# Join's transposed blocks in the tile that also holds the right side of the solve and the state sum, and a fourth buffer for second parts of weights

## Chip, cores and metric

The kernel runs on one core of a Trainium2 chip. A core has five engines that run side by side: TensorE (PE; its weight loads are PEld), VectorE (DVE), ScalarE (ACT), GpSimd (POOL) and SyncE (SP, which here issues DMAs only). Each takes its instructions in the order in which the built program lists them. The metric is the device time of one execution in microseconds (us), as a median of several runs.

## What is computed

A two-layer decoder trunk on x of 1024 tokens by 1024 channels, all in float32. The first layer mixes over time by the RWKV-7 recurrence, the second by sliding-window attention; each layer is followed by a squared-ReLU MLP with 4096 hidden channels. The change touches the recurrence:

```python
def step(S, inp):
    r_t, w_t, k_t, v_t, a_t, b_t = inp
    sa = jnp.einsum('bhvk,bhk->bhv', S, a_t)
    S = S * w_t[:, :, None, :] + sa[..., None] * b_t[:, :, None, :] + v_t[..., None] * k_t[:, :, None, :]
    y = jnp.einsum('bhvk,bhk->bhv', S, r_t)
    return S, y
...
def squared_relu_mlp(h, w1, w2):
    return jnp.square(jax.nn.relu(h @ w1)) @ w2
```

## The kernel before

**Products.** A float32 product of the projections, MLPs and attention is made of three products of parts (`mm3`, L132 to L136): each operand is split into a first part, rounded on ScalarE (L129), and a second part, the rest, subtracted on VectorE (L130). For a weight, `weight` (L265) loads 128x512 raw values into a tile with the tag `wr`, and writes the first part into a tile `wh` and the second into a tile `wl`. A tile tag has a fixed number of buffers (L45 to L47: 5 for `wr`, 4 for `wh`, 3 for `wl`), taken in turn: the next tile of a tag may be written once everything that reads the old tile in that buffer is done. An activation's two parts go to tiles `m2k`; in the projections each activation comes out of a mix of two tokens (`shifted`, L347, whose VectorE rows are L353 and L358 and write `relu`), and its second part is subtracted on VectorE or on GpSimd.

**Recurrence.** It is worked in chunks of 64 tokens. The 1024 tokens and 16 heads make 16 units of 128 tokens (two chunks, c = 0 and 1) by 8 heads (L806). A unit goes through these steps, whose order within the program is given by short strings (L53 to L55, L817):

- `prep` and `inner` (L574, L627) make decayed keys and the matrices of a chunk: AR, BK, and RT with XT, the blocks of a triangular matrix that has to be inverted. Of each 64x64 matrix, four 32x32 blocks, XT holds the transpose; its block at the second 32 rows and first 32 columns is not used by anybody.
- `solve` (L669) inverts the diagonal 32x32 blocks, 31 dependent pairs of steps on GpSimd (L680, L682), and brings the results through memory into RT (DMAs of L684, L689).
- `join` (L693) fills in the off-diagonal blocks: two VectorE transposes (L700), products on TensorE (L705), copies on ScalarE into the tile AT (L707), products (L711), copies into RT.
- `chunks` (L716) carries the state through the two chunks: products with the state SV (L743, L748), `pb` copied by ScalarE (L745), the solve's products with `pb` and RT (L752) copied into SV (L754), the sum of the state, `sn` (L757, L759), and from it SV for the second chunk (L762) and the state itself (L763).
- `finish` (L770) normalizes and stores.

`join` of a unit stands last in its string, behind `chunks` of the unit before it. But the build has a scheduler: it orders each engine's instructions by their priority and by when it reckons that their operands are ready, within what data and buffers allow. The recurrence is given priority (L810); the projections, and later the first MLP, supply the work around it.

**Stages** (times in the profile of before): projections with the first units up to about 656 us, the output product of the time mix to about 820 us, the first MLP with the last units to about 1230 us, then the queries and attention beside MLPs, and a pure MLP from about 2110 us to the end.

Of the kernel before, what the change touches and what calls it, by code (L numbers as in the profile page):

```python
# [10 lines left out]
F32 = mybir.dt.float32  # L11
# [8 lines left out]
P = 128  # L20
# [7 lines left out]
D = 64  # L28
L = 64
TB = 128  # L30
NC = TB // L
GP = 4
# [3 lines left out]
B = 32  # L36
# [7 lines left out]
M2K = 24  # L44
WR = 5  # L45
WH = 4
WL = 3  # L47
ROWS = 4
STG = 3
RELU = 3  # L50
# [24 lines left out]
class Trunk:  # L75
# [25 lines left out]
    def t(self, pool, tag, shape, dt=F32, bufs=1):  # L101
        return pool.tile(shape, dt, tag=tag, name=self.nm(tag), bufs=bufs)
# [162 lines left out]
    def weight(self, ap, shape, gain=None):  # L265
# [3 lines left out]
        nc.sync.dma_start(raw, ap)  # L269
        hi, lo = self.t(self.mp, "wh", shape, F32R, WH), self.t(self.mp, "wl", shape, F32R, WL)  # L270
        if gain is None:
# [103 lines left out]
    def lora_out(self, W2, u, off, dst, pt):  # L375
# [7 lines left out]
        for o in range(KT):  # L383
            if o % 4 == 0:
                raw = self.t(self.mp, "wr", [P, 512], F32, WR)
                for r0 in (0, 64):
                    nc.sync.dma_start(raw[r0:r0 + 64], W2[:, o * P:o * P + 512])
                wh, wl = self.t(self.mp, "wh", [P, 512], F32R, WH), self.t(self.mp, "wl", [P, 512], F32R, WL)
                nc.scalar.copy(wh, raw)
# [303 lines left out]
    def join(self, made):  # L693

        nc = self.nc
        AR, BK, RT, EL, bonus, XT, Xs = made
        n = NQ // 2
        sides = [(hp, self.sides(hp)[1].start, self.sides(hp)[2].start) for hp in range(2)]
        for hp, b, k in sides:
            nc.vector.transpose(XT[b:b + B, :, 0:B], RT[k:k + B, hp, :, 0:B])  # L700
        AT = self.t(self.rp, "AT", [P, n, B], F32)
        ps = self.turn().rearrange("p (q i) -> p q i", i=B)
        for q in range(n):
            for hp, b, k in sides:
                nc.tensor.matmul(ps[k + B:k + L, q], XT[b:b + B, q, B:], XT[b:b + B, q, 0:B], start=True, stop=True)  # L705
        for hp, b, k in sides:
            nc.scalar.copy(AT[k + B:k + L], ps[k + B:k + L, 0:n])  # L707
        ps = self.turn().rearrange("p (q i) -> p q i", i=B)
        for q in range(n):
            for hp, b, k in sides:  # L710
                nc.tensor.matmul(ps[k:k + B, q], AT[k + B:k + L, q], RT[k + B:k + L, hp, q, B:], start=True, stop=True)  # L711
        for hp, b, k in sides:
            nc.scalar.copy(RT[k:k + B, hp, :, B:], ps[k:k + B, 0:n])
        return AR, BK, RT, EL, bonus

    def chunks(self, blk, g, made):  # L716

        nc = self.nc
        t = lambda tag, shape, bufs=1, dt=F32: self.t(self.rp, tag, shape, dt, bufs)
        pt, t0 = PART[blk]  # L720
        AR, BK, RT, EL, bonus = made
        SV = t("SV", [P, NC, 2, GP, D])
        sides = [(hp, *self.sides(hp)[1:]) for hp in range(2)]
        heads = [(pi, *x) for pi in range(GP) for x in sides]
        dV = self.dV[pt][t0:t0 + TB, g * GH * D:(g + 1) * GH * D]
        for hp, bs, ks in sides:
            for c in range(NC):
                nc.sync.dma_start(SV[ks, c, hp], dV[c * L:(c + 1) * L].rearrange("l (r h d) -> l h r d", h=2, d=D)[:, hp])
            nc.vector.tensor_copy(SV[bs, 0, hp], self.state[g][bs])
        bv = t("bv", [P, NC, GH, D])  # L730
        nc.sync.dma_start(bv[L:].rearrange("l c h d -> l c (h d)"), dV.rearrange("(c l) d -> l c d", l=L))
        nc.gpsimd.tensor_tensor(bv[L:], bv[L:], bonus[L:].unsqueeze(3).broadcast_to([L, NC, GH, D]), ALU.mult)
        y = t("y", [P, GP, NC, L])

        def bank():
            return self.turn().rearrange("p (h d) -> p h d", d=D)[:, 0:GP]

        S = self.state[g]
        for c in range(NC):
            el = EL[:, :, c].unsqueeze(2).broadcast_to([P, GP, D])  # L740
            ps = bank()
            for pi, hp, bs, ks in heads:
                nc.tensor.matmul(ps[ks, pi], AR[:, hp, pi * NC + c, L:], SV[:, c, hp, pi], start=True, stop=True)  # L743
            pb = t("pb", [P, GP, D])
            nc.scalar.copy(pb, ps)  # L745
            py = bank()
            for pi, hp, bs, ks in heads:
                nc.tensor.matmul(py[bs, pi], SV[:, c, hp, pi], AR[:, hp, pi * NC + c, 0:L], start=True, stop=True)  # L748
            nc.scalar.copy(y[:, :, c], py)
            ps = bank()  # L750
            for pi, hp, bs, ks in heads:
                nc.tensor.matmul(ps[bs, pi], RT[ks, hp, pi * NC + c], pb[ks, pi], start=True, stop=True)  # L752
            for hp, bs, ks in sides:
                nc.vector.tensor_copy(SV[bs, c, hp], ps[bs])  # L754
            ps = bank()
            for pi, hp, bs, ks in heads:
                nc.tensor.matmul(ps[bs, pi], BK[:, pi * NC + c, hp], SV[:, c, hp, pi], start=True, stop=True)  # L757
            sn = t("sn", [P, GP, D])
            nc.vector.tensor_tensor(sn, ps, S, ALU.add)  # L759
            if c < NC - 1:  # L760
                for hp, bs, ks in sides:
                    nc.vector.tensor_tensor(SV[bs, c + 1, hp], sn[bs], el[bs], ALU.mult)  # L762
            nc.vector.tensor_tensor(S, sn, el, ALU.mult)  # L763
            py = bank()
            for pi, hp, bs, ks in heads:
                nc.tensor.matmul(py[bs, pi], SV[bs, c, hp, pi], RT[bs, hp, pi * NC + c], start=True, stop=True)
            nc.vector.tensor_tensor(y[:, :, c], y[:, :, c], py, ALU.add)
        return y, bv
# [355 lines left out]
```

## Time and profile before

| | us |
|---|---|
| median of 3 runs | 2679.01 |
| lowest and highest | 2678.21, 2679.69 |
| the profiled execution | 2679.98 |
| its span, first to last instruction | 2678.3 |
| TensorE busy | 2541.7 (95%) |
| VectorE busy | 1700.6 (63%) |
| ScalarE busy | 1306.1 (49%) |
| GpSimd busy | 621.2 (23%) |
| mean granted TensorE clock | 0.972 of full |

Busy times are sums over one execution on the chip. An engine that waits is not busy; the trace says for most waits which instruction's end released it, and "issue" where it shows none. TensorE's clock has two levels, 1.2 and 2.4 GHz; a granted clock of 0.97 over a stretch is the mean of the two there.

### The profile page before, as it was taken

The numbers are of one execution on the slowest core, as the hardware profiler recorded it, in microseconds if no ns is written. First come the engines' busy times: TensorE is split into PE (matmuls) and PEld (weight loads), VectorE is DVE, ScalarE is ACT, GpSimd is POOL, SyncE is SP. The second block draws the span as 40 slices with busy tenths as digits, with TensorE's granted clock in tenths as the row PEclk, the third lists the DMA queues.
The fourth block names the chain that finished last, engine by engine and source line by source line (L and its number), as shares of the span: only waits on it lengthen the run. The fifth ranks groups of instructions, "written<-read, shape, count | busy, mean of one in ns | idle before, by whom it ended". The sixth has DMA issues, their size and how long they took to land.

```text
span 2678.3 us, 43154 instructions
## 1 busy us (share of the span) xinstructions
PE 2541.7 (95%) x15166; PEld 2054.0 (77%) x15166; DVE 1700.6 (63%) x3235; ACT 1306.1 (49%) x2702; POOL 621.2 (23%) x1221
## 2 busy tenths in 40 slices
PE   6978988998889999999999999999999999999999
PEld 4767766766767777777887888888888888888887
DVE  8578778656666666645567885445899644444433
ACT  5555566464444444333455665335666533434342
POOL 6176744740454444420010000001000000000000
PEclk9989989899889999999999999999999999999999
DMA  5656643654644444333424454342446433333332
GB/s 177 196 173 177 184 115 113 179 143 151 177 105 114 120 122 117 109 107 119 140 87 151 126 153 123 95 154 89 138 142 196 123 103 96 121 91 105 96 99 95
DMA packets 440635, 349.64 MB, mean 131 GB/s; under 512 B 97105, under 2 KB 360417, under 8 KB 440417
## 3 DMA queue, kind: packets, MB, share of 16 engines
q1 hardware_dynamic: 423008, 344.77, 43.1%
q10 hardware_dynamic: 17408, 2.10, 0.5%
q8 instruction: 120, 1.97, 0.3%
q14 instruction: 99, 0.80, 0.1%
HBM read 280.71 MB, written 57.67 MB: 126 GB/s over the span
## 4 chain that ended last, share of the span: by engine, by line
PE 50%; DVE 3%; DMA 2%; ACT 1%; issue 1%; SPq 0%; DVEq 0%; ACTq 0%
PE big L134 16%; PE big L135 16%; PE big L136 16%; DMA dS<-sc 1%; DMA row<-dS 1%; DVE wl L130 0%; DVE sc L975 0%; DVE sc L978 0%; DMA wr<-in_mlp_w 0%; PE sm L1001 0%; PE sq L955 0%; PE sm L1002 0%; PE sq L956 0%; PE big L252 0%; SPq L983 0%
## 5 line engine op out<-in xcount | busy, mean ns | idle before, releaser
L129 ACT CAST wh<-wr 128x512 fp32r<-128x512 f32 x741 | 458.0, 620 | 853.4 <-PE big L136 435.5
L130 DVE TENSOR_TENSOR wl<-wr,wh 128x512 fp32r<-128x512 f32 x741 | 527.3, 716 | 474.5 <-issue 223.4
L134 PE MATMUL big<-m2k,wh 128*128 128x512 f32 (+3 forms) x1528 | 578.6, 381 | 12.2 <-ACT m2k L129 4.6
L135 PE MATMUL big<-wl,m2k 128*128 128x512 f32 (+1 forms) x1472 | 578.4, 394 | 9.4 <-DVE wl L130 7.6
L135 PE MATMUL big<-m2k,wh 128*128 128x512 f32 (+2 forms) x1528 | 572.7, 376 | 6.4 <-POOL m2k L130 4.3
L136 PE MATMUL big<-m2k,wl 128*128 128x512 f32 (+2 forms) x1528 | 571.8, 377 | 5.1 <-DVE wl L130 5.1
L136 PE MATMUL big<-wh,m2k 128*128 128x512 f32 (+1 forms) x1472 | 566.9, 392 | 3.0 <-POOL m2k L130 3.0
L134 PE MATMUL big<-wh,m2k 128*128 128x512 f32 (+1 forms) x1472 | 512.1, 394 | 11.3 <-ACT m2k L129 7.7
L134 PEld LDWEIGHTS big<-m2k,wh 128*128 128x128 f32 (+1 forms) x1528 | 292.0, 192 | 76.1 <-issue 6.3
L135 PEld LDWEIGHTS big<-wl,m2k 128*128 128x128 f32 x1472 | 281.3, 191 | 72.2 <-DVE wl L130 13.5
L136 PEld LDWEIGHTS big<-m2k,wl 128*128 128x128 f32 (+1 forms) x1528 | 292.0, 191 | 58.1 <-DVE wl L130 7.7
L135 PEld LDWEIGHTS big<-m2k,wh 128*128 128x128 f32 (+1 forms) x1528 | 291.7, 191 | 57.8 <-POOL m2k L130 7.0
L134 PEld LDWEIGHTS big<-wh,m2k 128*128 128x128 f32 x1472 | 279.9, 191 | 73.0 <-ACT m2k L129 9.1
L136 PEld LDWEIGHTS big<-wh,m2k 128*128 128x128 f32 x1472 | 280.4, 191 | 59.3 <-POOL m2k L130 3.6
L680 POOL TENSOR_TENSOR tmp<-Xs,TT 128x60 f32<-128x60 f32 (+24 forms) x496 | 197.2, 398 | 143.2 <-DMA Xs<-dXs 106.7
L130 DVE TENSOR_TENSOR m2k<-relu,m2k 128x512 fp32r<-128x512 f32 (+1 forms) x200 | 135.1, 678 | 119.6 <-ACT m2k L129 119.2
L682 POOL TENSOR_TENSOR TT<-TT,tmp 128x60 f32<-128x60 f32 (+24 forms) x496 | 195.1, 393 | 37.8
L129 ACT CAST m2k<-relu 128x512 fp32r<-128x512 f32 (+1 forms) x272 | 146.6, 545 | 45.8 <-DVE relu L353 33.4
L322 DVE TENSOR_TENSOR b<-b,big 128x512 f32<-128x512 f32 x192 | 124.7, 680 | 8.8 <-PE big L136 8.2
L223 POOL TENSOR_TENSOR ss<-ss,mhalf 128x4 f32<-128x4 f32 (+1 forms) x10 | 8.9, 888 | 453.8 <-DVE ss L222 453.8
L223 POOL TENSOR_TENSOR qn<-qn,mhalf 128x8 f32<-128x8 f32 x16 | 27.1, 1692 | 373.8 <-DVE qn L222 290.4
L314 ACT ACTIVATE relu<-relu 128x512 f32<-128x512 f32 x128 | 80.9, 633 | 3.5
(229 smaller groups left out, 3089.6 us busy)
## 6 DMA issues: line engine op xcount, KB each, us to landing
wr<-in_mlp_w SPq DMA_DIRECT2D x512, 256.0 KB, 2.7
wr<-in_a_w_rkv SPq DMA_DIRECT2D x144, 256.0 KB, 3.2
ld<-dP SPq DMA_DIRECT2D x16, 1024.0 KB, 6.8
dS<-sc SPq DMA_DIRECT2D x28, 512.0 KB, 2.8
row<-dS SPq DMA_DIRECT2D x112, 128.0 KB, 3.0
dP<-stg SPq DMA_DIRECT2D x64, 128.0 KB, 3.4
AR<-RA SPq DMA_DIRECT2D x32, 256.0 KB, 4.4
Xs<-dXs SPq DMA_DIRECT2D x64, 128.0 KB, 2.7
```

Source lines behind the costliest of these rows:

```text
L129: self.nc.scalar.copy(hi, src)
L130: (engine or self.nc.vector).tensor_tensor(lo, src, hi.bitcast(F32), ALU.subtract)
L134: mm(ps, ah, bh, start=start, stop=False)
L135: mm(ps, ah, bl, start=False, stop=False)
L136: mm(ps, al, bh, start=False, stop=stop)
L223: nc.gpsimd.tensor_tensor(dst, dst, self.mhalf[:, :n], ALU.pow)
L314: nc.scalar.activation(r, r, AF.Square)
L322: nc.vector.tensor_tensor(v, v, ps[tt], ALU.add)
L680: nc.gpsimd.tensor_tensor(v, Xs[:, k:k + 1, k + 1:].broadcast_to([P, m, n]), TT[:, 0:m, k:k + 1].broadcast_to([P, m, n]), ALU.mult)
L682: nc.gpsimd.tensor_tensor(TT[:, 0:m, k + 1:], TT[:, 0:m, k + 1:], v, ALU.add)
```

## The change

Three edits. `join` writes its two transposes into a new tile TX, with the tag `pb`, of which there is one buffer; the sum `sn` of `chunks` gets the same tag, so `pb`, the sum and TX follow each other in one buffer. The transposes are no longer put into XT; the products of L705 (now L707) read TX and XT. AT is not a tile of its own any more but the unused block of XT. The two tags that are gone (`sn` and AT, 1 KB in each partition each) make room for a fourth `wl` buffer of 2 KB. Lines from L700 on stand one or two further down in the change (L700 is L701, L743 is L745, L759 is L761, L762 is L764).

```diff
-WL = 3
+WL = 4
...
+        TX = self.t(self.rp, "pb", [P, n, B], F32)
         for hp, b, k in sides:
-            nc.vector.transpose(XT[b:b + B, :, 0:B], RT[k:k + B, hp, :, 0:B])
-        AT = self.t(self.rp, "AT", [P, n, B], F32)
+            nc.vector.transpose(TX[b:b + B], RT[k:k + B, hp, :, 0:B])
+
+        AT = XT[:, :, 0:B]
         ps = self.turn().rearrange("p (q i) -> p q i", i=B)
         for q in range(n):
             for hp, b, k in sides:
-                nc.tensor.matmul(ps[k + B:k + L, q], XT[b:b + B, q, B:], XT[b:b + B, q, 0:B], start=True, stop=True)
+                nc.tensor.matmul(ps[k + B:k + L, q], XT[b:b + B, q, B:], TX[b:b + B, q], start=True, stop=True)
...
-            sn = t("sn", [P, GP, D])
+            sn = t("pb", [P, GP, D])
```

**What it does to the order.** First VectorE, in the unit of the first of five alike (beside the first MLP). Before, from the first chunk's sum on; RT_9682 and XT_9683 belong to the next unit, SV_9559 and states to this one:

```order
L759 TENSOR_TENSOR sn_9611<-sq_9602,states 128x256
L700 STREAM_TRANSPOSE XT_9683<-RT_9682 32x8x32
L767 TENSOR_TENSOR y_9569<-y_9569,sq_9616 128x4x64
L762 TENSOR_TENSOR SV_9559<-sn_9611,EL_8584 64x256 x2
L763 TENSOR_TENSOR states<-sn_9611,EL_8584 128x256
L130 TENSOR_TENSOR wl_12471<-wr_12468,wh_12470 128x512
L700 STREAM_TRANSPOSE XT_9683<-RT_9682 32x8x32
L130 TENSOR_TENSOR wl_12497<-wr_12494,wh_12496 128x512
```

Now, from the same sum on:

```order
L761 TENSOR_TENSOR pb_9611<-sq_9602,states 128x256
L764 TENSOR_TENSOR SV_9559<-pb_9611,EL_8584 64x256 x2
L765 TENSOR_TENSOR states<-pb_9611,EL_8584 128x256
L769 TENSOR_TENSOR y_9569<-y_9569,sq_9616 128x4x64
L130 TENSOR_TENSOR wl_12471<-wr_12468,wh_12470 128x512
```

SV and the state now follow the sum at once. The transposes stand further on, here from the second chunk's sum:

```order
L761 TENSOR_TENSOR pb_9667<-sq_9658,states 128x256
L130 TENSOR_TENSOR wl_12551<-wr_12548,wh_12550 128x512
L769 TENSOR_TENSOR y_9569<-y_9569,sq_9670 128x4x64
L731 COPY SV_9974<-states 64x256 x2
L648 TENSOR_TENSOR RT_10097<-sm_10099,maskg 64x256
L765 TENSOR_TENSOR states<-pb_9667,EL_8584 128x256
L648 TENSOR_TENSOR RT_10097<-sm_10100,maskg 64x256
L701 STREAM_TRANSPOSE pb_9933<-RT_9682 32x256 x2
L592 COPY EL_10266<-ec_10262 128x8
L130 TENSOR_TENSOR wl_12574<-wr_12571,wh_12573 128x512
```

Both transposes now stand directly behind the second chunk's last use of its sum. Of the 16 joins, 8 had their first transpose ahead of the second chunk's sum before (the seventh, the eighth and the last six); in the change none has.

Second, TensorE at the same unit in the change, where the second chunk's first products begin:

```order
L135 MATMUL big_12412<-wl_12435,m2k_12318 128x512
L136 MATMUL big_12412<-wh_12434,m2k_12319 128x512
L745 MATMUL sq_9626<-SV_9559,AR_9265 64x64
L134 MATMUL big_12410<-wh_12452,m2k_12362 128x512
L745 MATMUL sq_9626<-SV_9559,AR_9265 64x64 x7
L750 MATMUL sq_9637<-AR_9265,SV_9559 64x64 x8
```

Between the last product of L759, which the first chunk's sum reads, and the first of L745 stand the eight small products of L768 and 20 products of the MLP.

Third, VectorE near the start of the program, in the projections (`relu` is the mix of two tokens, `wl` a weight's second part), as a piece of the difference:

```order
 L477 COPY hlast<-b_8_188 128x8
+L130 TENSOR_TENSOR wl_372<-wr_369,wh_371 128x512
 L468 COPY b_367_1551<-hlast 128x8
 L353 SCALAR_TENSOR_TENSOR relu_250<-m2k_221,vec,b_8_188 128x256
```

The fourth `wl` of the program moved ahead of six rows of L353, and the fifth moved up alike. Such shifts by a few rows go through all of the program.

## Rows read from the trace of the kernel before

**Rows 1.** The page: busy time, share of the span and instructions of each engine.

```profile
PE 2541.7 (95%) x15166; PEld 2054.0 (77%) x15166; DVE 1700.6 (63%) x3235; ACT 1306.1 (49%) x2702; POOL 621.2 (23%) x1221
```

**Rows 2.** Busy times in stages: stretch, length, PE, PEld, DVE, ACT, POOL, clock, DMA.

```profile
0.00:656.00 656.00, 572.18 (x4429) 444.86 (x4430) 479.23 (x935) 372.48 (x832) 331.13 (x642) 0.92 0.55 160
...
820.00:1130.00 310.00, 294.83 (x2295) 234.10 (x2294) 203.48 (x376) 122.44 (x238) 134.96 (x309) 0.99 0.42 114
...
2110.00:2678.00 568.00, 562.90 (x2488) 464.02 (x2486) 242.74 (x373) 218.81 (x365) 1.01 (x1) 1.00 0.33 100
```

**Rows 3.** Waits of TensorE from 820 to 1130 us: total, times, longest.

```profile
PE sq L743 <- issue: 12.0, 5, 2.8
```

**Rows 4.** VectorE in order of time, 1085 to 1097 us: start, length, idle before.

```profile
1085.62 0.69 DVE L130 TENSOR_TENSOR m2k<-relu,m2k 128x512 fp32r<-128x512 f32 x1 [1.54 <-ACT m2k L129]
1086.34 0.42 DVE L759 TENSOR_TENSOR sn<-sq,states 128x256 f32<-128x256 f32 x1
1093.97 0.43 DVE L700 STREAM_TRANSPOSE XT<-RT 32x256 f32<-32x256 f32 x1 [7.21 <-DMA RT<-dTT]
...
1094.78 0.86 DVE L762 TENSOR_TENSOR SV<-sn,EL 64x256 f32<-64x256 f32 x2
```

**Rows 5.** TensorE in order of time, at the same unit.

```profile
1095.29 0.24 PE L743 MATMUL sq<-SV,AR 128*64 128x64 f32 x1 [2.79 <-issue]
...
1132.89 0.69 PE L705 MATMUL sq<-XT 32*32 32x32 f32 x32
```

**Rows 6.** VectorE in order of time, 602 to 605 us.

```profile
602.71 0.43 DVE L700 STREAM_TRANSPOSE XT<-RT 32x256 f32<-32x256 f32 x1 [6.39 <-DMA RT<-dTT]
...
604.67 0.87 DVE L754 COPY SV<-sq 64x256 f32<-64x256 f32 x2
```

**Rows 7.** TensorE in order of time, at 605 us.

```profile
605.14 0.33 PE L757 MATMUL sq<-SV,BK 128*64 128x64 f32 x2 [1.72 <-DVE SV L754]
```

**Rows 8.** VectorE at the end of the second chunk of the unit of rows 4.

```profile
1107.98 0.42 DVE L763 TENSOR_TENSOR states<-sn,EL 128x256 f32<-128x256 f32 x1
```

**Rows 9.** GpSimd in order of time, the last steps of the solve.

```profile
1085.74 0.69 POOL L680 TENSOR_TENSOR tmp<-Xs,TT 128x42 f32<-128x42 f32 x1
1086.51 0.27 POOL L682 TENSOR_TENSOR TT<-TT,tmp 128x42 f32<-128x42 f32 x1
1086.86 0.26 POOL L680 TENSOR_TENSOR tmp<-Xs,TT 128x35 f32<-128x35 f32 x1
...
1089.68 0.21 POOL L682 TENSOR_TENSOR TT<-TT,tmp 128x8 f32<-128x8 f32 x1
```

**Rows 10.** The tile tmp, 820 to 1130 us: ns, shortest/median/longest.

```profile
L680 POOL TENSOR_TENSOR tmp<-Xs,TT x142: 208/294/1292, 820.5 to 1129.4; 128x60 f32<-128x60 f32 x12, 128x48 f32<-128x48 f32 x10, 128x28 f32<-128x28 f32 x10, 128x54 f32<-128x54 f32 x9
```

**Rows 11.** Waits of TensorE over the whole span: total, times, longest.

```profile
PE big L134 <- ACT m2k L129: 12.3, 5, 5.1
...
PE big L135 <- DVE wl L130: 7.6, 11, 1.2
PE big L136 <- DVE wl L130: 5.1, 6, 2.3
...
PE big L135 <- DVE wl L275: 1.8, 2, 0.9
...
PE big L394 <- DVE wl L390: 0.7, 1, 0.7
```

**Rows 12.** Waits of TensorE in the first 100 us.

```profile
PE big L135 <- DVE wl L130: 5.5, 8, 1.2
```

**Rows 13.** Busy times near the start (columns as in rows 2).

```profile
28.00:56.00 28.00, 22.50 (x88) 15.33 (x88) 28.00 (x35) 15.56 (x36) 23.11 (x24) 1.00 0.45 133
```

**Rows 14.** The tile wl on VectorE, 0 to 656 us: ns, shortest/median/longest.

```profile
L130 DVE TENSOR_TENSOR wl<-wr,wh x163: 482/693/2031, 12.0 to 653.5; 128x512 fp32r<-128x512 f32 x154, 128x480 fp32r<-128x480 f32 x6, 128x320 fp32r<-128x320 f32 x3
```

**Rows 15.** Busy times in two later stretches of 65 us (columns as in rows 2).

```profile
886.00:951.00 65.00, 62.12 (x481) 49.12 (x478) 43.66 (x80) 26.42 (x52) 28.77 (x63) 0.97 0.42 114
951.00:1016.00 65.00, 61.76 (x500) 48.95 (x498) 44.09 (x81) 26.45 (x53) 30.01 (x67) 1.00 0.44 119
```

## The prediction, before the change was run

> **What bounds the kernel now.** I read the page first. TensorE is busy for 95% of the span and VectorE for 63% [rows 1]. The busy times by stage place what is lost [rows 2]: from 0 to 656 us (projections) TensorE is idle for 84 us at a mean clock of 0.92; in the last 568 us it is idle for 5 us. So a change can only win before about 1300 us, by closing gaps in TensorE's work. There is one regular series of gaps: from 820 to 1130 us, while the first MLP runs beside the recurrence, TensorE is idle for 15.2 us in all, and 12.0 us of that is five waits in front of L743, the first product of a chunk [rows 2, 3]. Those rows name no releaser ("issue"), so I looked at VectorE around the last of them [rows 4]. It finishes the state sum of a unit's first chunk at 1086.76, and the next row in its order is join's first transpose for the *next* unit, which waits 7.21 us for the DMA that brings the solved blocks. Behind it stand the two instructions (L762) that write SV for the second chunk. They need nothing but the sum, yet start at 1094.78; TensorE, which had reached L743, resumes at 1095.29 after a gap of 2.79 us [rows 5]. So these gaps are order on VectorE, not work.
>
> **The change part by part.**
>
> *TX in the tile of the sums.* TX has the tag of the sums and one buffer, so no transpose may be written while a sum of the unit before it is still to be read; its last reader is L763 on VectorE itself. The scheduler must thus put both transposes behind the second chunk's L763, as the order of the change shows. In 8 of the 16 joins they stood ahead of it before, the five with gaps among them. With SV straight behind the sum, SV is there some 1.3 us after the sum begins (0.42 for it, 0.86 for the two copies [rows 4]); in the new order 20 products of the MLP stand on TensorE between the end of L759 and L745, some 4.5 us at the 0.226 us for each in the pure MLP (562.90 us for 2488 [rows 2]), so TensorE should not wait. I take the five gaps as gone: **-12.0 us**. The full amount reaches the end, since from 820 us on TensorE has little other idle time. One earlier join has the same fault on another instruction: at 602.71 the transposes that had waited for the DMA hold up the copy at L754, and TensorE stands 1.72 us at L757 [rows 6, 7]: **-1.7 us**.
>
> What does the wait cost in its new place? Shifted forward, the second chunk ends its sums at 1086.8 + (1107.98 - 1094.78) = 1100.0 [rows 4, 8], and the solved blocks had landed by 1093.97: 6 us to spare. The join's products start only at 1132.89 [rows 5], so they are not delayed. Nor does sharing cost a wait across engines: `pb` of a chunk follows join's first products in TensorE's order anyhow, and the sum follows the products that read `pb`. Zero, covered by these distances.
>
> The spare has an enemy: VectorE no longer stands idle under the end of the solve. While VectorE subtracted two tiles in SBUF (the L130 row of [rows 4]) a 128x42 step on GpSimd took 0.69 us, the next step of that size 0.27 [rows 9]. The ten steps behind the sum, 1086.86 to 1089.89, take 0.26 falling to 0.21 us each [rows 9], 2.3 in all; at 0.69 each they take 6.9 and the blocks land 4.6 us later, still inside the 6 us. At the longest step seen, 1.29 us [rows 10], they would not. The Trainium skill, GPSIMD Engine Reference, section 1. Specifications, says that GpSimd shares its SBUF interfaces with VectorE and contends with VectorE instructions that have two SBUF inputs; by that rule the wait comes back, which is the second rival. The trace agrees as to the slowing, not as to its size.
>
> *AT in the unused block of XT.* Same two copies, same sizes, and XT has two buffers; it is held until join's second products instead of the first, with the unit's next user two units away. Zero.
>
> *Fourth `wl` buffer.* No instruction is added. It lets VectorE split a weight one tile further ahead. TensorE's direct waits on `wl` bound what that can win: 7.6 + 5.1 + 1.8 + 0.7 = 15.2 us [rows 11]. Of these at least 5.5 us lie in the first 100 us [rows 12], where VectorE has no idle time from 28 to 56 us [rows 13]: there a tile made earlier pushes the activations behind it later, and I give nothing for it. Of the other 9.7 us I take a third, **-3.2 us**, because several stand behind a VectorE that was held by something else. Bounds: 0 and -15.2; and below, since an order that favours weights can also starve the activations (last rival).
>
> *The clock.* Two stretches of 65 us that hold one of the five gaps each ran at 0.97 and at 1.00 [rows 15]: gaps of this size did not pull the clock down as a rule, and I take 0 for it. The Trainium skill, TensorE: Matmul & The Clock Gate, section HAM oscillation, holds that idle gaps of TensorE also drop its clock; by that the closed gaps would give back more, an estimate of 2 us (3% of 65) wherever it happens, or 10 us over five. In the projections the mean clock is 0.92, and one hundredth more over 656 us is 6.6 us [rows 2]; I keep that for the low end.
>
> *Sum.* -12.0 - 1.7 - 3.2 = -16.9 us. The profiled execution took 2679.98 us (span 2678.3), 1.0 above the median of 2679.01. So 2663.1 by it, **2662 us** as a median.
>
> **The rivals.**
>
> *The fourth buffer pays more.* All 15.2 us of waits on `wl` go, and some clock with them: 2679.0 - 12.0 - 1.7 - 15.2 = 2650, or 2644 with the 6.6 us kept for the clock. For it: in the projections VectorE is busy for 479 of 656 us and splits 163 tiles of weights at L130 [rows 2, 14], and a run-ahead of one tile evens out a queue. Against it: little of its idle time stands before exactly those waits. Chance 0.15.
>
> *The wait moves instead of going.* The solve, slowed by a busy VectorE, lands later than the second chunk's sums. The transposes then hold up what stands behind them, weights and the sums of the MLP, and the 12.0 us come back there: 2679.0 - 1.7 - 3.2 = 2674. It decides at a landing more than 6 us later. For it the two step times; against it the 4.6 us at 0.69 each. Chance 0.12.
>
> *Slower: weights ahead of activations.* The order of the whole projection stage is redone, and at its start the change puts splits of weights before the L353 rows that feed TensorE through ScalarE and GpSimd. Where VectorE has no pause each split that comes too early costs one of 0.69 us; TensorE already waits 12.3 us at L134 for such activations, the largest single entry [rows 11]. It takes 2684.4 - 2662 = 22 us, 32 of the 163 tiles [rows 14], to come out slower by over 0.2%; at one tile in four, 41, the time is 2690. For it: this stage has the most idle time and gaps of up to 5.1 us on activations. Against it: the same instructions must all run, and a weight that comes early is not wasted. Chance 0.12.
>
> That the change does not do what it says can be left out: the order shows it.
>
> **How the numbers follow.** My forecast has 0.61 (2655 to 2668). 0.2% is 5.4 us, about what a measurement of this kernel can tell from no change: faster is below 2673.7, slower above 2684.4. Faster takes the forecast, the first rival and a part of the second (0.02): 0.78. Within 0.2%: the rest of the second, 0.10, and 0.01 from the slow one where it is mild: 0.11. Slower: 0.11. The range goes from 2644, the low end of the first rival, to 2680: it leaves out the slow case and a few hundredths below.
>
> **What would show it.** Right: from 820 to 1130 us no wait of TensorE at L745 worth more than 1 us in total; both transposes behind L765, with little or no wait for the DMA; SV within 2 us of the sum; the stage some 12 us shorter. The waits of TensorE on `wl` should sum to about 12 us, and the idle time before 656 us stay within 10 us of 84. Wrong: the transposes still waiting several us for the DMA with gaps of TensorE behind them, or the projection stage longer or shorter by over 10 us, which would make the redone order, not the join, the larger term.

## The result, and the profile after

| | before | after |
|---|---|---|
| median, us | 2679.35 | 2642.57 |
| lowest and highest | 2678.21, 2682.8 | 2641.87, 2644.27 |
| span of the profiled execution | 2678.3 | 2640.2 |
| mean granted TensorE clock | 0.972 | 0.973 |

The ratio is 0.986, 95% interval 0.9846 to 0.9874: 36.8 us less. The forecast was 2662, the range 2644 to 2680. The sign was right; the size was not, and the median lies 1.4 us under the low end.

The page of after, busy times (against [rows 1]):

```profile
PE 2522.8 (96%) x15166; PEld 2046.1 (77%) x15166; DVE 1704.5 (65%) x3235; ACT 1304.2 (49%) x2702; POOL 618.9 (23%) x1221
```

TensorE runs the same 15166 products, is busy for 18.9 us less and idle for 19.2 us less (span less busy time: 136.6 before, 117.4 after). So half of the gain is not idle time at all, and for that the prediction had no term in its sum.

Busy times by stage of after (columns as in [rows 2]). The stage 774 to 1286 runs from the end of the time mix to the second MLP and holds the first MLP beside the recurrence:

```profile
0.00:656.00 656.00, 570.49 (x4458) 445.25 (x4459) 487.59 (x941) 376.43 (x843) 326.64 (x642) 0.92 0.56 164
...
774.00:1286.00 512.00, 510.51 (x3772) 409.58 (x3772) 320.41 (x576) 212.05 (x407) 182.34 (x406) 1.00 0.43 123
```

The same stage of before:

```profile
782.00:1320.00 538.00, 519.94 (x3796) 415.16 (x3795) 323.38 (x583) 214.83 (x412) 184.53 (x409) 0.99 0.41 118
```

538 us became 512. Idle time fell from 18.1 to 1.5 us, and busy time by 9.4 us. 24 products fewer account for some 3 us of that; the clock, 0.99 to 1.00, for most of the rest. In the pure MLP at the end TensorE is busy for 562.6 of 568 us, as before [rows 2].

VectorE of after, in order of time, in the unit that answers to [rows 4] and at its second chunk:

```profile
1051.04 0.42 DVE L761 TENSOR_TENSOR pb<-sq,states 128x256 f32<-128x256 f32 x1 [1.31 <-PE sq L759]
...
1051.98 0.94 DVE L764 TENSOR_TENSOR SV<-pb,EL 64x256 f32<-64x256 f32 x2
...
1072.73 0.42 DVE L765 TENSOR_TENSOR states<-pb,EL 128x256 f32<-128x256 f32 x1
1073.19 0.90 DVE L701 STREAM_TRANSPOSE pb<-RT 32x256 f32<-32x256 f32 x2
```

SV for the second chunk is there 1.9 us after its sum began, against 9.3 [rows 4]. The transposes follow the second chunk's L765 and wait for nothing. SyncE had issued the loads of the solved blocks long before:

```profile
1058.93 2.35 SPq L689 DMA_DIRECT2D RT<-dTT  x4
```

With 1.9 us from issue to landing, as the trace has it for these four, they are there by 1063.2, 10 us ahead. From 770 to 1324 us the trace of after has no wait of TensorE at L745; the nearest to it is one of 0.2 us at L759.

Waits of TensorE of after on second parts of weights, over the whole span (against [rows 11]); two other waits of TensorE, from the same view; and two of VectorE's own waits in front of `wl` to 680 us:

```profile
PE big L135 <- DVE wl L130: 3.1, 5, 1.2
PE big L136 <- DVE wl L130: 2.3, 4, 1.0
...
PE big L393 <- DVE m2k L381: 7.6, 3, 4.5
PE sq L570 <- ACT wide L568: 7.1, 1, 7.1
...
DVE wl L130 <- ACT wh L129: 81.5, 55, 8.0
DVE wl L130 <- PE big L136: 1.9, 2, 1.4
```

In before, VectorE's rows of the same view:

```profile
DVE wl L130 <- PE big L136: 27.4, 20, 2.7
DVE wl L130 <- issue: 20.5, 13, 3.9
DVE wl L130 <- ACT wh L129: 17.6, 13, 5.0
```

TensorE's waits on `wl` fell from 15.2 to 5.7 us (3.1, 2.3 and one of 0.3 at L394), and VectorE now waits for ScalarE's first parts rather than for TensorE to release a second part.

**A measure for what follows.** For each product of TensorE: the time from its start to the start of the next one, less the median of that time over all runs for products of its kind and shape. Summed over a stage this *excess* holds idle time and slowed products alike. Stages end at the last product of L438 (projections), at the 32nd product of L252 (time mix done, first MLP begins) and at the 33rd (second MLP begins). In us:

| run | projections | time mix | MLP with recurrence | rest | sum |
|---|---|---|---|---|---|
| before | 133.7 | 33.2 | 29.1 | 26.0 | 222.0 |
| e1 (order of before, 3 `wl`) | 136.0 | 32.5 | 30.8 | 29.7 | 229.0 |
| e5 (order of before, 3 `wl`) | 133.5 | 32.8 | 28.8 | 27.5 | 222.5 |
| e2 (order of before, 4 `wl`) | 121.8 | 31.8 | 32.7 | 25.3 | 211.5 |
| e3 (new order, 3 `wl`) | 132.6 | 27.9 | 5.8 | 28.7 | 195.1 |
| after (new order, 4 `wl`) | 125.4 | 30.1 | 6.1 | 22.1 | 183.8 |
| e6 (after again) | 121.4 | 31.3 | 6.4 | 23.9 | 183.1 |

From before to after it falls by 38.2, the change of the span: 23.0 in the MLP with the recurrence, 8.3 in the projections, 3.1 and 3.9 in the other two. The MLP column tells the two orders apart in every run of this document: 28.8 to 32.7 in the four with the order of before, 3.1 to 7.7 in the fourteen with the new one.

Each row is one profiled execution, so a few microseconds between two rows tell nothing: after and e6 are one kernel and differ by 4.0 us in the projections and 1.8 in the rest, and the profiled execution of e1 was its slowest (2686.95 us, median 2681.61), that of e2 its second fastest (2668.34, median 2674.13). A pause right behind the last product of a stage counts to the next stage; before, e1, e3 and e5 have one of some 4 us behind the projections, e2, after and e6 have none. One of the four executions of e3 took 6891.75 us; its ratio below leaves that one out, its median does not (of the other three it is 2656.7).

### The profile page after: what moved, and what is told of

Its sections match the earlier page's. It is cut to its first block, busy times and chain, and to the rows that moved or that the text cites. A ratio compares the mean times of both kernels' runs of the same rounds, so it can differ in the third digit from the quotient of the medians.

```text
span 2640.2 us, 42811 instructions
## 1 busy us (share of the span) xinstructions
PE 2522.8 (96%) x15166; PEld 2046.1 (77%) x15166; DVE 1704.5 (65%) x3235; ACT 1304.2 (49%) x2702; POOL 618.9 (23%) x1221
## 4 chain that ended last, share of the span: by engine, by line
PE 80%; DVE 6%; POOL 5%; DMA 4%; ACT 2%; issue 2%; SPq 0%; POOLq 0%; ACTq 0%; DVEq 0%
PE big L134 23%; PE big L136 23%; PE big L135 23%; POOL tmp L680 2%; POOL TT L682 2%; DMA ld<-dP 1%; PE sm L642 1%; DVE wl L130 1%; DVE relu L353 1%; PE sq L759 1%; PE sq L768 1%; PE sq L745 1%; PE big L394 0%; ACT wh L129 0%; DMA Xs<-dXs 0%
## 5 line engine op out<-in xcount | busy, mean ns | idle before, releaser
L135 PE MATMUL big<-wl,m2k 128*128 128x512 f32 (+1 forms) x1472 | 577.6, 393 | 3.1 <-DVE wl L130 3.1
L135 PE MATMUL big<-m2k,wh 128*128 128x512 f32 (+3 forms) x1528 | 569.3, 373 | 5.3 <-POOL m2k L130 4.0
L136 PE MATMUL big<-m2k,wl 128*128 128x512 f32 (+3 forms) x1528 | 570.8, 375 | 2.4 <-DVE wl L130 2.3
L134 PE MATMUL big<-wh,m2k 128*128 128x512 f32 (+1 forms) x1472 | 559.8, 394 | 11.3 <-ACT m2k L129 8.6
L136 PE MATMUL big<-wh,m2k 128*128 128x512 f32 (+1 forms) x1472 | 564.5, 390 | 0.0
L134 PEld LDWEIGHTS big<-m2k,wh 128*128 128x128 f32 (+1 forms) x1528 | 288.6, 190 | 72.9 <-ACT m2k L129 5.8
L134 PEld LDWEIGHTS big<-wh,m2k 128*128 128x128 f32 x1472 | 279.5, 191 | 71.9 <-ACT m2k L129 10.2
L135 PEld LDWEIGHTS big<-m2k,wh 128*128 128x128 f32 (+1 forms) x1528 | 289.1, 189 | 58.8 <-POOL m2k L130 6.7
L135 PEld LDWEIGHTS big<-wl,m2k 128*128 128x128 f32 x1472 | 280.6, 191 | 63.1 <-DVE wl L130 6.1
L680 POOL TENSOR_TENSOR tmp<-Xs,TT 128x60 f32<-128x60 f32 (+24 forms) x496 | 192.8, 389 | 165.7 <-DMA Xs<-dXs 129.1
L682 POOL TENSOR_TENSOR TT<-TT,tmp 128x60 f32<-128x60 f32 (+24 forms) x496 | 198.9, 401 | 37.8
L130 DVE TENSOR_TENSOR m2k<-relu,m2k 128x512 fp32r<-128x512 f32 (+1 forms) x200 | 136.6, 687 | 78.6 <-ACT m2k L129 78.0
L322 DVE TENSOR_TENSOR b<-b,big 128x512 f32<-128x512 f32 x192 | 123.9, 680 | 27.6 <-PE big L136 27.2
```

Source lines behind the costliest of these rows:

```text
L130: (engine or self.nc.vector).tensor_tensor(lo, src, hi.bitcast(F32), ALU.subtract)
L134: mm(ps, ah, bh, start=start, stop=False)
L135: mm(ps, ah, bl, start=False, stop=False)
L136: mm(ps, al, bh, start=False, stop=stop)
L322: nc.vector.tensor_tensor(v, v, ps[tt], ALU.add)
L680: nc.gpsimd.tensor_tensor(v, Xs[:, k:k + 1, k + 1:].broadcast_to([P, m, n]), TT[:, 0:m, k:k + 1].broadcast_to([P, m, n]), ALU.mult)
```

## The experiments

Theory A: the gain in the MLP stage is the order on VectorE, which the shared tile forces, and the fourth `wl` adds its own in the projections. Rivals: the gain comes from where the blocks lie, or from weights alone. Ratios are to the kernel before, with 95% intervals; diffs are against after.

**e1, e2: the blocks back in place, with three and with four `wl`.** The sum keeps the tag `pb`, and AT the block of XT.

```diff
-WL = 4
+WL = 3        # e1 only
-        TX = self.t(self.rp, "pb", [P, n, B], F32)
+        TX = XT[:, :, 0:B]
```

> Transposes stay in XT (8 of 16 joins with the first transpose ahead of the second chunk's state sum, as in the kernel before), the sum shares the tile of pb, AT lies in XT, 3 buffers of wl. Theory A (the order of join behind the chunks carries the gain, with its full price of 22 to 26 us in the MLP stage, and wl the rest): within 5 us of the kernel before, 2674 to 2684, and the five gaps at L743 are there with 10 to 14 us. Theory B (the fourth wl buffer carries more than the order): also within 5 us of before. Theory C (any new order of the program gains or loses tens of us by chance): off by over 8 us either way.

> As the run before, with the fourth wl buffer, so the whole change but for the transposes' tile. Theory A: 2664 to 2670 (10 to 15 us faster than the kernel before), with the gaps in front of L743 still there in the first MLP. Theory B: 2650 to 2658, over 20 us faster. Theory C: anywhere from 2650 to 2690.

e1: 2681.61 us, ratio 1.0003 (0.9991 to 1.0014): no gain. So sharing by the sum and AT in XT cost and bring nothing. e2: 2674.13, ratio 0.9967 (0.9955 to 0.998): 7 to 9 us faster than before, 4 us short of what theory A expected. In both the transposes stand again ahead of the next SV in eight joins of e1 and nine of e2. TensorE's waits at L745 over the whole span, first e1:

```profile
PE sq L745 <- issue: 12.8, 6, 3.0
```

then e2:

```profile
PE sq L745 <- issue: 17.7, 6, 4.3
```

**e3, e4: the new order with three `wl`; e4 also with six raw buffers.**

```diff
-WL = 4
+WL = 3
-WR = 5
+WR = 6        # e4 only
```

> The change with 3 buffers of wl: only the transposes follow the chunks. Theory A: 2652 to 2659 (20 to 27 us faster than the kernel before), no gaps in front of the second chunk's first products between 780 and 1290 us, that stage 22 to 27 us shorter than before, and the projections as long as before to 4 us. Theory B: 2664 to 2670. Theory C: anywhere.

> As the run before, but the 2 KB go to a sixth buffer of wr (raw weights) instead of a fourth of wl. Theory A and B: as the run with TX and 3 wl to 3 us, since TensorE waits on wl and wh, not on raw weights. Theory C: differs from it by over 8 us.

e3: 2657.54, ratio 0.9905 (0.9881 to 0.993). e4: 2655.71, 0.9899 (0.9873 to 0.9925). From e1 to e3, one line, 24 us by the medians and 26 by the ratios; the fourth `wl` is in neither. A sixth raw buffer moves nothing.

**e5: the blocks in a tile of their own.** The same move out of XT as the change, with nothing shared.

```diff
-WL = 4
+WL = 3
-        TX = self.t(self.rp, "pb", [P, n, B], F32)
+        TX = self.t(self.rp, "TX", [P, n, B], F32)
```

> The blocks of TX in a tile of their own, not shared with the sums; three second parts of weights. The two transposes then stand ahead of the next chunk's SV in eight joins again, as in the kernel before. If the gain of the join is the order that the shared tile forces, the time is that of the kernel before within 0.2% (ratio 0.998 to 1.002), with some 12 us of TensorE's waits in front of L745 back. If it comes from moving the blocks out of the tile of the solve (the left side free earlier, other addresses), the time is that of the shared tile with three second parts, ratio about 0.990.

2684.55, ratio 1.0005 (0.9995 to 1.0015). VectorE of e5, in order of time, has the picture of [rows 4] again:

```profile
1084.68 0.42 DVE L761 TENSOR_TENSOR pb<-sq,states 128x256 f32<-128x256 f32 x1
1092.38 0.43 DVE L701 STREAM_TRANSPOSE TX<-RT 32x256 f32<-32x256 f32 x1 [7.28 <-DMA RT<-dTT]
```

So the move does nothing; the shared tile, and so the order, does it all. Theory A stands for this part.

**e6: after again.** No edit.

> The changed kernel unchanged, beside the others of this call. If order and fourth second part simply add, the ratio is 0.986 to 0.988, some 8 to 12 us below the shared tile with three second parts (0.9905 in the earlier call); if part of the fourth buffer's gain was chance of that call, it is 0.989 or more.

2640.98, ratio 0.9847 (0.9834 to 0.9859), a little better than the 0.986 to 0.988 that adding them gave. Against e3 the fourth `wl` is worth 0.45% (after) or 0.58% (e6), 12 to 16 us; in place, e1 to e2, 0.36%, 10 us. e3 ran in another series than after and e6, so 12 to 16 is less certain than 10, which comes from two runs of one series.

**e7, e8, e9: a fifth part, paid for with one raw buffer, and the raw buffer alone.**

```diff
-WR = 5
+WR = 4        # e7, e8, e9
-WL = 4
+WL = 5        # e7 only
-WH = 4
+WH = 5        # e8 only
```

> The changed kernel with five second parts of weights, paid for with one raw weight buffer (five to four). With four, VectorE's own wait before splitting a weight stands on ScalarE's rounding of the first part (81 us of it) and hardly on TensorE's release of the second (under 2 us). If the first part is now what holds the queue, a fifth second part does nothing: the changed kernel's time within 3 us. If the second part still limits, 3 to 8 us less.

> The changed kernel with five first parts of weights, paid for with one raw weight buffer (five to four). If ScalarE waits for a free first part and VectorE for ScalarE, this takes what is left of TensorE's direct waits on weights (5.7 us) and evens the start: 3 to 8 us less than the changed kernel. If the raw buffers limit instead, or ScalarE is late by its own work, no change within 3 us, or some us more for the missing raw buffer.

> The changed kernel with four raw weight buffers instead of five and nothing else: what the two runs with a fifth part paid for it. If the missing raw buffer is what made them slower, this is 5 to 10 us above the changed kernel, most of it before 680 us. If raw buffers don't matter (six of them instead of five moved nothing), it is the changed kernel's time within 3 us, and a fifth part itself made the order worse.

e7: 2650.18, ratio 0.9876 (0.9862 to 0.989). e9: 2648.92, 0.9876 (0.9859 to 0.9893). So the raw buffer costs 4 to 8 us (against after and e6), and a fifth `wl` gives nothing. e8: 2645.98, 0.9857 (0.9844 to 0.987): the expected gain on after did not come. Against e9, which has the same raw buffers, e8 is 3 to 5 us faster, but the intervals overlap.

**e10 to e12: a fifth first part with all five raw buffers, paid for elsewhere.**

```diff
-WH = 4
+WH = 5
-RELU = 3
+RELU = 2      # e10, e12
-STG = 3
+STG = 2       # e11, e12
-WL = 4
+WL = 5        # e12 only
```

> The changed kernel with five first parts of weights and all five raw buffers, paid for with the third relu buffer. If VectorE's waits on ScalarE's first parts (80 us) are what the fourth second part ran into, 4 to 10 us less than the changed kernel, in the projections. If those waits are only where VectorE's spare time now stands, no change within 3 us.

> The same five first parts, paid for with the third staging buffer instead of the third relu buffer. As the run with two relu buffers if the first part is what counts, 4 to 10 us less than the changed kernel; if the two differ by more than 5 us, the order that the scheduler happens to make is worth as much as a buffer.

> Five first and five second parts, paid for with one relu and one staging buffer. If the two kinds of parts limit each other in turn, this has TensorE's waits on weights under 3 us and is the fastest, 6 to 12 us below the changed kernel. If four of each is enough, no change within 3 us, or some us more for the two buffers given up.

All missed. e10: 2659.53, ratio 0.9919 (0.9904 to 0.9934). e11: 2671.97, 0.9966 (0.9952 to 0.998). e12, expected fastest: 2695.24, 1.0051 (1.0037 to 1.0065), slower than before. Its waits on `wl` are all but gone, 1.5 us in all, the longest of them here:

```profile
PE big L136 <- DVE wl L130: 0.7, 1, 0.7
```

yet in the first 680 us its clock is 0.87, where after has 0.92 (columns as in [rows 2]):

```profile
0.00:680.00 680.00, 582.73 (x4452) 453.75 (x4453) 473.09 (x926) 364.50 (x817) 332.16 (x642) 0.87 0.53 152
```

Its TensorE is busy for 5.4 us less than that of e3 (below), and has done 126 products fewer. In e10 to e12 TensorE is at half clock for 150 to 181 us of the projections, in after for 102.

**e13, e14: the new order with three `wl`, and the memory of the fourth given to others.**

```diff
-WL = 4
+WL = 3
-WH = 4
+WH = 5        # e13 only
-RELU = 3
+RELU = 4      # e14 only
```

> The changed join, three second parts of weights as before, and the tile given to a fifth first part. If the gain of the fourth buffer is that VectorE no longer waits for TensorE to release a second part, this does nothing: the time of the changed join alone, ratio 0.990 to 0.991. If any further tile for weights does as well, 0.985 to 0.987.

> The changed join, three second parts, and the tile given to a fourth relu row. As above: 0.990 to 0.991 if the gain belongs to the second part; below 0.988 if it is a matter of any buffer and the order it makes.

e13: 2676.91, ratio 0.9979 (0.9966 to 0.9992), 20 us *more* than e3 for one more buffer, and in neither of the cases expected. e14: 2649.64, 0.9879 (0.9863 to 0.9895), by a hair in the second case (below 0.988), "any buffer and the order it makes"; but its interval overlaps e3's, so the two cases are not told apart. Stretches of the first 680 us, e3:

```profile
0.00:680.00 680.00, 588.16 (x4578) 455.06 (x4578) 493.75 (x955) 387.55 (x863) 342.08 (x644) 0.93 0.56 162
```

and e13:

```profile
0.00:680.00 680.00, 591.79 (x4520) 462.35 (x4521) 484.63 (x944) 374.37 (x841) 338.25 (x642) 0.89 0.54 155
```

e13 is *busier* and gets 58 products less far: its clock is lower.

**e15, e16: one relu row, one staging buffer given up, alone.**

```diff
-RELU = 3
+RELU = 2      # e15
-STG = 3
+STG = 2       # e16
```

> The changed kernel with two relu rows instead of three. If giving up that buffer is what cost the run with five first parts its time, this is slower than the changed kernel by 10 to 20 us (ratio 0.990 to 0.993). If the fifth first part cost it, the changed kernel's time within 4 us.

> The changed kernel with two staging buffers instead of three. If that buffer is what cost, slower than the changed kernel by 20 to 35 us (ratio 0.994 to 0.998), the end of the projections 25 to 35 us later; if the fifth first part, the changed kernel's time within 4 us.

e15: 2649.18, ratio 0.9871 (0.9855 to 0.9886); e16: 2663.44, 0.9927 (0.9915 to 0.9939). Both lie between the cases expected. If the losses add, of what e10 lost the relu row is the smaller part (0.24% of 0.72%, against e6), and the fifth first part the larger; in e11 the staging buffer is the larger (0.80% of 1.19%). None of the versions tried clearly beats after.

## Why the prediction was right in kind and wrong in size

**The order: right as a mechanism, sized at 13.7 us where it was 24 to 26 (e1 to e3), or 29 to 32 beside four `wl` (e2 to after and e6).** What it named as signs of the order came true: no wait at L745 in the MLP stage, transposes behind L765 with no wait for the DMA, SV within 2 us of the sum. e1, e3 and e5 show that the order alone does it. The step that failed is "I take the five gaps as gone: -12.0 us". It priced the five waits that the trace lists, not the stage that holds them. With the fourth `wl`, sized too small as well (below), this covers the miss of 19 us. From e5 to e3 the excess there falls by 23.0 us:

- 12 us are the listed waits (12.1 in e5, none in e3);
- 3 us are other idle time of TensorE in that stage, which fell by 15.0 in all (17.8 to 2.8);
- 5 us are clock: 10.2 us of the stage ran at half speed in e5, none in e3, and half of that is lost;
- some 3 us are not placed.

A further 5 us come from the time mix just before it, of which the prediction had nothing: 2 of idle time and most of the rest in products at half clock, for what reason is not shown. In the projections, where the gap of 1.7 us was to go, the excess hardly moves (133.5 to 132.6). One sign against the forecast came as well, a projection stage over 10 us shorter: its last product ends at 665.4 us in after, at 676.7 before. It is at 675.8 in e3, so this part is the fourth `wl`, and the join stays the larger term.

**The clock: "I take 0 for it" was wrong.** [rows 15] showed 0.97 in one stretch with a gap and 1.00 in another, and the prediction took the second as the rule. The place is plain in e2, whose gaps are the longest. Three stretches of it, before a gap of 3.4 us in front of L745, right behind that gap, and after:

```profile
935.00:944.50 9.50, 9.50 (x69) 7.65 (x68) 3.17 (x6) 5.23 (x9) 6.71 (x21) 1.00 0.03 4
947.40:954.00 6.60, 5.59 (x39) 4.47 (x40) 5.18 (x11) 1.36 (x3) 0.00 (x0) 0.50 0.39 106
954.00:1012.00 58.00, 58.00 (x457) 46.33 (x457) 37.84 (x71) 25.33 (x49) 30.18 (x66) 1.00 0.40 115
```

2.4 GHz without a pause, then a gap, then 1.2 GHz, then 2.4 again. In e2 this follows four of the five gaps at L745 (those of 2.4 to 4.3 us), in e1 three of five, in before two of five, in e5 two of five; in the MLP stages of after and e3, without such gaps, it never happens, and in e8, which has the new order, it happens once, behind a gap of 2.5 us in front of L759. So a gap does not always pull the clock down, but a gap of over a microsecond went ahead of each fall in this stage. The Trainium skill, TensorE: Matmul & The Clock Gate, section HAM oscillation, says that idle gaps throttle the clock, so that the cold products are paid on top of the wait; the traces agree, with some 5 us on top of the 15 us of idle time that e5 has over e3. The prediction's estimate by that rule, up to 10 us over five gaps, contained the 5 that it then struck out.

**The fourth `wl`: "a third, -3.2 us" was wrong; it gave 10 to 16.** The prediction's ceiling was 15.2, all of TensorE's waits on `wl`. They fell by 9.5 us, but idle time before the end of the projections did not follow: 76.7 us before, 77.7 after, 75.8 in e6. Other waits took their place: up to there those at L393 and L570, shown above with 7.6 and 7.1 us, had 1.9 and 1.1 before. The excess of the projections, with the order held, falls by 14.2 us in place (e1 to e2; the medians of the whole kernels are only 7.5 apart, since e1's profile was a slow one) and by 7.2 beside the new order (e3 to after). Of that 4.5 and 2.0 us are idle time, 5.6 and 0.6 the extra length of products at half clock, 4.1 and 4.6 that of products at full clock. So the listed waits were no measure of the term, in either direction. How the fourth `wl` gains where the idle time stays the same is open.

Of its gain, 4 to 7 us (e1 to e2, e3 to after) fell in a place that the prediction had closed: "a change can only win before about 1300 us". In the rest column the runs with three `wl` have 26.0 to 30.4 (before, e1, e3, e4, e5, e13, e14), those with four and four first parts 21.9 to 25.3 (e2, after, e6, e9, e15, e16); e7, with five, has 27.2. A fifth first part beside four `wl` takes this column down further, to 17.1 to 18.9 (e8, e10, e11), while it costs in the projections: the best number of buffers differs by stage. That it is the second part that counts is shown against the first part (e13) and the raw tile (e4); against any other tile it is not, since e14, with a relu row in its place, came out halfway. "I give nothing" for the first 100 us was too strict too: TensorE's waits on `wl` there fell from 5.5 [rows 12] to 3.1 at L135.

**The zeros: right.** AT in XT and the sum in `pb` cost nothing (e1). The solve's steps hold their length beside a busy VectorE: the median of `tmp` from 800 to 1110 us is 297 ns, before it was 294 [rows 10]. Over the whole stage the same 372 steps on `tmp` (L680 and L682) took 146.3 us before and 146.5 after.

```profile
L680 POOL TENSOR_TENSOR tmp<-Xs,TT x162: 206/297/1227, 800.4 to 1109.7; 128x60 f32<-128x60 f32 x17, 128x66 f32<-128x66 f32 x11, 128x54 f32<-128x54 f32 x11, 128x48 f32<-128x48 f32 x11
```

The wait did not move, so the second rival falls.

**The rivals.** The first, "the fourth buffer pays more", came true in its price and not in its way (9.5 of the 15.2 us of waits went, and the idle time stayed), on top of an order worth twice its price. The slower one, weights ahead of activations, did not happen in after, but one buffer further something like it does: with a fifth first part and three `wl` (e13) VectorE waits 57 us for TensorE to release a second part to 720 us, where e3 has 33, and what stands behind it on VectorE waits too. TensorE's waits sum to much the same (95 and 94 us), but half-speed products cost 59.9 us beyond their usual length, where e3 has 35.8. That this is the run-ahead of weights was not isolated; e8, with the fifth first part but one raw buffer less, did not lose, which would fit it. Why the same idle time lies differently for the clock stays open.

## What to carry to other kernels

A wait on an in-order engine can cost more than the gap that the trace lists behind it (here 12 us listed, 24 to 26 gained): measure the stage against the same work without gaps (here the pure MLP's pace), and price the clock behind each gap. To move an instruction behind another that a scheduler puts ahead, let both share a buffer: the dependence gives the order, here at no cost, since the wait had 10 us of slack. A buffer more is not a gain by itself: of the tiles tried, a fourth second part won 10 to 16 us and a fifth nothing; a fifth first part lost 20 us beside three `wl` (e3 to e13), 10 to 13 beside four (e15 to e10, e16 to e11), and nothing with one raw buffer less (e9 to e8). Test each alone.

## What the runs showed of the hardware that was not expected

The length of a gap does not tell whether the clock falls behind it: of the five at L743 or L745, in before those of 1.9 and 2.3 us were followed by half clock and those of 2.5 to 2.8 us were not; in e5, the same order of these waits, those of 2.7 and 2.9 us were and those of 1.8 to 2.5 us were not. In e1 two almost equal gaps, of 2.67 and 2.75 us, stand one unit apart: the first was followed by half clock, the second was not. Runs with nearly the same idle time of TensorE differ by over 20 us in the projections, almost all of it through the clock: e3 and e13 have 79.7 and 82.8 us of it to the end of the projections, and 92 and 157 us at half clock, of 676 and 698.
